# Prompt attention: both heads of a pair in one item, scores in the row halves of TensorE's array, V products alternating between its column halves

## The chip, the cores and the metric

One core of one Trainium2 chip runs the whole program. The metric is the device time of one execution in microseconds; lower is better. Everything is float32. The large projections run as pairs of the faster float32 form (`fp32r`): every number is split into its first bits and the rest, and three products replace one. The products of attention take plain float32 operands; the trace shows one such matmul as two rows, each with a weight load of its own.

## The reference, cut to what matters

Two layers of a streaming encoder are run on 512 prompt frames and on 8 running streams of 16 new frames (the samples). The change touches prompt attention in the second layer: 8 heads of 64 features, every 64-frame chunk attending to itself and to the chunks before it (all 8 of them at most, so over 512 frames the band is the whole causal triangle of chunks), with a bias by relative position.

```python
def band_attention_prompt(q, k, v, rel_bias):
    ...
    scores = jnp.einsum('bcqhd,bckhd->bchqk', chunks(q), kb).astype(jnp.float32) * (D_HEAD_DIM ** -0.5)
    scores = scores + bias.transpose(1, 0, 2, 3)[None].astype(jnp.float32)
    scores = jnp.where((kpos >= 0)[None, :, None, None, :], scores, NEG_INF)
    probs = jax.nn.softmax(scores, axis=-1).astype(v.dtype)
    out = jnp.einsum('bchqk,bckhd->bcqhd', probs, vb)
    return out.reshape(bn, S, D_WIDTH)
```

## The kernel before

All matrix work goes to TensorE. A recorder, `Weave`, runs Python generators and issues their instructions in an order that it works out from estimated TensorE times: a generator yields a number of ns that its next TensorE work has to wait, or an event. Lower priority numbers go first. The tile framework below it may still move an instruction where a buffer isn't free. On the chip each engine takes its instructions in that fixed order.

`odd_mixer` is the second layer's mixer. Its main task (priority 9) projects V, then the pooling inputs, then for each pair of heads j = 0 to 3 K and Q by feature (`kq_proj(j)`: 4 groups of 24 fp32r matmuls with 256 or 384 columns, in `wst`), and then the output projection in two pieces (`out_chunk`: 3 and 5 units of 128 features). Three streams (priority 1) fill in: they take prompt items, and after the event `room` (all K and Q are projected) sample items.

A prompt item before is one head `h` of a pair `j` and one query tile `qt` of 128 frames, 32 items in all, with n = (qt + 1) x 128 keys:

1. scores: one matmul over all 128 rows of the array. `kT` holds both heads' K, 64 features each; `qz` holds Q twice, with the other head's rows zero (L1060, L1061, L1069), so that the product over 128 rows is that of one head;
2. softmax: VectorE adds the bias (up to 256 columns) and takes the maximum, ScalarE takes the exponential and its sum, VectorE scales;
3. qt + 1 transposes of 128 x 128, into the scores' bank, and a copy to `pt` by ScalarE;
4. V products: qt + 1 matmuls with 64 output features, into partitions 64h to 64h + 63 of the pair's bank `pos[j]`, which is a column half of the array.

When a pair's 8 items are done its bank is split into `cat[4 + j]` for the output projection. A sample item has scores and V products in four column strips of 32; its cached K and V (1 MB each) are loaded by SyncE (SP) at L1137 into the pool `xpool` of 7 buffers, in order, each load waiting for a buffer to come free. The eight PSUM banks are shared by all.

Of the kernel before, what the change touches and what calls it, by code (L numbers as in the profile page):

```python
# [10 lines left out]
AF = mybir.ActivationFunctionType  # L11
# [34 lines left out]


class Weave:
    """Issues generators' instructions in the order in which TensorE can take them.

    A generator yields None where another may go on, a number of ns that its next
    TensorE work has to wait, or an Event to wait for.
    """

    def __init__(self):
        self.now = 0.0
# [28 lines left out]


class Ordered:
    """An engine whose instructions keep the program's order while on is set."""

    on = False  # L90

# [14 lines left out]
def trunk_kernel(  # L106
# [57 lines left out]
    def mm(out, lhsT, rhs, start, stop, n, share=1, more=False):  # L164
        fast = lhsT.dtype == F32R
        W.now += PASS * (max(n, 256) if fast else 4 * n / share) + 2
        nc.tensor.matmul(out, lhsT=lhsT, rhs=rhs, start=start, stop=stop, skip_group_check=more)  # L167
# [11 lines left out]
    def bank(shape=(P, 512)):  # L179
        return psp.tile(list(shape), F32, tag="ps", name=nm("ps"))  # L180

    def t4(shape):
        return t4p.tile(list(shape), F32, tag="t4", name=nm("t4_"))

    def t2(shape):
        return t2p.tile(list(shape), F32, tag="t2", name=nm("t2_"))

    def st(n=1):
        return stp.tile([P, n], F32, tag="st", name=nm("st"))
# [17 lines left out]
        return rawp.tile([P, 5, 512], F32, tag="raw", name=nm("raw"))  # L207

    def fetch(srcs):
        """Yields the rows of srcs in turn, loaded two by two."""  # L210
        for i, src in enumerate(srcs):
            if i % 2 == 0:
                w = raw()[:, :4, :].rearrange("p (h a) c -> p h (a c)", h=2)
                nc.sync.dma_start(out=w[:, 0, :], in_=src)
                if i + 1 < len(srcs):
                    nc.sync.dma_start(out=w[:, 1, :], in_=srcs[i + 1])
            yield w[:, i % 2, :]
# [17 lines left out]
        return r  # L235

    class Norm:
        """1 / sqrt(mean of squares + EPS), the squares in one or two parts."""

        def __init__(self):  # L240
            self.ms = None
# [14 lines left out]
            return rsqrt(self.ms)  # L256

    class Normed:
        """The normed rows by feature, each number as its first 12 bits and the rest."""

        def __init__(self, gain):
            self.gain = gain
# [18 lines left out]
            return [x[:, c] for x in self.part(k)]  # L281

    class Quarters:
        """The same in quarters (feature half, row half) and with Winograd's four sums of them."""

        def __init__(self, gain, rows=False):
            self.gain = gain
# [111 lines left out]
    def group_cols(g):  # L399
        return slice(0, GA) if g == 0 else slice(GA, NT)  # L400

    def wst(X, hl, g):
        for t in ((0, 1), (2, 3, 4))[g]:
            yield X.ev[t]
        cols = group_cols(g)
        n = cols.stop - cols.start
        ps = bank()
        for k in range(NK):
            c = slice(k * P, (k + 1) * P)
            xh, xl = X.part(k)  # L410
            mm(ps[:, :n], hl[:, 0, c], xh[:, cols], k == 0, False, n)
            mm(ps[:, :n], hl[:, 0, c], xl[:, cols], False, False, n)
            mm(ps[:, :n], hl[:, 1, c], xh[:, cols], False, k == NK - 1, n)
            if k % 4 == 3:
                yield
        return ps[:, :n]
# [78 lines left out]
        return PostNorm(gpost, src, dst, after if X is not None else None)  # L495

    class Seven:
        """Two units of 128 output features with seven quarter products for eight.

        [A11 A12; A21 A22] times [B11 B12; B21 B22], the rows in halves, the features in  # L500
        halves, and the two units as the two column blocks.
        """

        def __init__(self, one, two, X):
            self.X = X
# [59 lines left out]
                    yield  # L565

    class GateUp(Seven):
        """Gate and up of 128 hidden features and their product."""

        def __init__(self, layer, f, X):  # L570
            super().__init__(wgate[layer, f], wup[layer, f], X)
# [20 lines left out]
            split((self.hid[:, 0, HT:], self.hid[:, 1, HT:]), up)  # L592

    class Units(Seven):
        """Two units by themselves."""

        def __init__(self, one, two, X):
            super().__init__(one, two, X)
# [10 lines left out]
            act.copy(out=self.out[0][:, HT:], in_=a)  # L609

    class Plain:
        """Two units of 128 output features, all eight quarter products as they are."""

        def __init__(self, one, two, X):
            self.X = X
# [95 lines left out]
    def even_mixer(X, hls):  # L711
# [56 lines left out]
        cat = {}  # L768

        def pairs(todo):  # L770
            """The pairs of units in todo, each with its weights made ready before the work on the last."""
            made = []

            def make():
                i, j, _ = todo[len(made)]
                p = (PlainUnits if (i, j) in DIRECT else Units)(ev_t[i], ev_t[j], X)
                p.prepare()
                made.append(p)

            make()  # L780
            for n, (_, _, use) in enumerate(todo):
                yield from made[n].steps()
                if n + 1 < len(todo):
                    make()
                yield from use(*made[n].out)
# [147 lines left out]
    def odd_mixer(X):  # L933
# [121 lines left out]
        def kq_proj(j):  # L1055
            hk = unit(feed)
            hq = unit(feed)
            kT = t2([P, NT])
            qz = t4([P, 2, NP])
            nc.gpsimd.memset(qz[64:128, 0, :], 0.0)  # L1060
            nc.gpsimd.memset(qz[0:64, 1, :], 0.0)  # L1061
            for g in range(2):
                cols = group_cols(g)
                pk = yield from wst(X, hk, g)
                act.copy(out=kT[:, cols], in_=pk)
                pq = yield from wst(X, hq, g)
                for h in range(2):
                    r = slice(64 * h, 64 * h + 64)
                    act.mul(out=qz[r, h, g * GA : (g + 1) * GA], in_=pq[r, :GA], mul=0.125)  # L1069
                    if g == 1:  # L1070
                        dve.tensor_scalar(
                            out=qs[r, j, :, h, :],
                            in0=pq[r, GA:].rearrange("p (b s) -> p b s", s=LS),
                            scalar1=0.125,
                            scalar2=None,
                            op0=ALU.mult,
                        )
            nc.gpsimd.tensor_copy(out=ks[:, j, :], in_=kT[:, NP:])
            nc.sync.dma_start(out=nkp[j], in_=kT[:, :NP])
            nc.sync.dma_start(out=nks[j], in_=ks[:, j, :])  # L1080
            kq[j] = (kT, qz)
            W.signal(kq_ev[j], 1500)

        def prompt_stream(items):
            for j, qt, h in items:
                yield kq_ev[j]
                kT, qz = kq[j]
                hd = 2 * j + h
                n = (qt + 1) * P
                nb_ = min(n, 256)  # L1090
                s = bank()
                mm(s[:, :n], qz[:, h, qt * P : (qt + 1) * P], kT[:, :n], True, True, n)
                dve.tensor_tensor(
                    out=s[:, n - nb_ : n],
                    in0=s[:, n - nb_ : n],
                    in1=bias[hd // 4][:, hd % 4, 256 - nb_ :],
                    op=ALU.add,
                )
                m = row_max([s[:, :n]])
                pr = t2([P, NP])  # L1100
                sm = st()
                act.activation(out=pr[:, :n], in_=s[:, :n], func=AF.Exp, bias=m, accum_out=sm)
                ri = st()
                dve.reciprocal(out=ri, in_=sm)
                dve.tensor_scalar(out=pr[:, :n], in0=pr[:, :n], scalar1=ri, scalar2=None, op0=ALU.mult)
                yield 1800 + 3.2 * n
                for kt in range(qt + 1):
                    flip(s[:, kt * P : (kt + 1) * P], pr[:, kt * P : (kt + 1) * P])
                pt = t2([P, NP])
                act.copy(out=pt[:, :n], in_=s[:, :n])  # L1110
                yield 400 + n
                if j not in pos:
                    pos[j] = bank()
                po = pos[j]
                for kt in range(qt + 1):
                    mm(
                        po[64 * h : 64 * h + 64, qt * P : (qt + 1) * P],
                        vt(kt)[:, hd * 64 : hd * 64 + 64],
                        pt[:, kt * P : (kt + 1) * P],
                        kt == 0,  # L1120
                        kt == qt,
                        P,
                        2,
                    )
                done[j] += 1
                if done[j] == 8:
                    ct = cat[4 + j] = hid_tile()
                    split((ct[:, 0, :NP], ct[:, 1, :NP]), po)
                    W.signal(prompt_done[j], 2000)
                yield  # L1130
# [77 lines left out]
                    W.signal(sample_done, 500)  # L1208
                yield

        prompt_items = iter([(j, qt, h) for j in range(4) for qt in range(4) for h in range(2)])
        sample_items = iter(range(NB))
        room = Event()

        def stream(i):
            yield from prompt_stream(prompt_items)
            yield room
            yield from sample_stream(sample_items)

# [179 lines left out]
```

## Time and profile before

| what | value |
|---|---|
| median of 3 runs | 1335.15 us (1334.96 to 1335.39) |
| span of the profiled execution | 1333.4 us |
| TensorE (PE) busy, share of the span | 1309.9 us, 98% |
| VectorE (DVE) busy | 890.7 us, 67% |
| ScalarE (ACT) busy | 618.5 us, 46% |
| K/Q projections with prompt items, 719 to 798 us | PE busy 78.89 of 79 us |
| rest of attention with the first piece of the output projection, 798 to 857 us | PE busy 57.04 of 59 us |

The span runs from the first to the last instruction of the program; the median is 1.75 us above it. PE's busy time is the union of its matmuls, whose ends are modelled, so what one matmul costs is read from start to start and not from its length.

### The profile page before, as it was taken

The page shows a single profiled execution, that of the slowest core. Times are in us where ns is not written, and L with a number is a line of the kernel's source. Part 1 is how long each engine was busy: PE and PEld are TensorE (multiplying, and loading weights), DVE is VectorE, ACT ScalarE, POOL GpSimd, SP SyncE. Part 2 cuts the span into 40 slices and gives each one's busy share as a digit, 9 for nine tenths or more (in the row PEclk, how much of TensorE's full clock was granted, in tenths as well). Part 3 has the DMA queues.
Part 4 walks back from the last instruction along what each step waited for, and adds up shares of the span by engine and source line. Part 5 has one row for each costly group of instructions (what it writes and reads, how often), then busy time and mean ns, then how long its engine had stood idle before and what let it go on. Part 6 is the DMA issues. An engine that isn't in the chain of part 4 may idle for free.

```text
span 1333.4 us, 20064 instructions
## 1 busy us (share of the span) xinstructions
PE 1309.9 (98%) x8060; PEld 1190.9 (89%) x8060; DVE 890.7 (67%) x1452; ACT 618.5 (46%) x1134; POOL 60.7 (5%) x119
## 2 busy tenths in 40 slices
PE   7999999999999999999999999999999999999997
PEld 5998989989899998998798886789999898998996
DVE  6985779837576674777556446579646575864866
ACT  5644546535253451554434445456545251551551
POOL 2200101000000000001121000010000000000000
PEclk9999999999999999999999999999999999999999
DMA  7212353212122122145346125642312121221233
GB/s 246 72 64 80 105 205 118 97 62 95 64 95 96 63 95 79 64 151 178 138 151 233 68 75 219 248 165 80 127 64 96 62 95 64 96 97 46 96 127 126
DMA packets 45966, 150.12 MB, mean 113 GB/s; under 512 B 6577, under 2 KB 8497, under 8 KB 45873
## 3 DMA queue, kind: packets, MB, share of 16 engines
q1 hardware_dynamic: 45872, 148.84, 30.7%
q8 instruction: 63, 1.03, 0.3%
q14 instruction: 31, 0.25, 0.1%
HBM read 133.57 MB, written 15.26 MB: 112 GB/s over the span
## 4 chain that ended last, share of the span: by engine, by line
PE 86%; DVE 5%; issue 3%; ACT 2%; DMA 2%; POOL 1%; SPq 0%; DVEq 0%; POOLq 0%; ACTq 0%
PE ps L167 85%; DVE t L99 3%; PE ps L171 1%; DMA xbuf<-t 1%; POOL st L234 1%; DMA raw<-in_dram 1%; ACT t L99 1%; DVE q L99 1%; ACT q L99 1%; DVE x L99 1%; DVE st L99 0%; ACT ps L99 0%; ACT f L99 0%; POOL t L751 0%; SPq L380 0%
## 5 line engine op out<-in xcount | busy, mean ns | idle before, releaser
L167 PE MATMUL ps<-x,q 128*128 128x320 f32 (+2 forms) x4884 | 729.2, 310 | 1.2 <-DVE q L99 1.0
L167 PEld LDWEIGHTS ps<-x,q 128*128 128x128 f32 x4884 | 718.0, 188 | 4.9 <-DVE q L99 2.2
L167 PE MATMUL ps<-q,hid 128*128 128x512 f32 x1800 | 417.6, 391 | 0.5 <-DVE hid L99 0.3
L99 ACT CAST q<-raw 128x1024 fp32r<-128x1024 f32 (+1 forms) x278 | 269.8, 978 | 298.3 <-PE ps L167 248.3
L99 DVE TENSOR_TENSOR q<-raw,q 128x1024 fp32r<-128x1024 f32 (+1 forms) x278 | 313.8, 1132 | 136.5 <-ACT q L99 131.7
L167 PEld LDWEIGHTS ps<-q,hid 128*128 128x128 f32 x1800 | 335.4, 188 | 70.4 <-DVE hid L99 1.0
L99 ACT COPY t<-ps 128x320 f32<-128x320 f32 (+3 forms) x304 | 135.6, 452 | 187.7 <-PE ps L167 169.3
L99 DVE TENSOR_TENSOR t<-ps,t 128x512 f32<-128x512 f32 (+2 forms) x164 | 100.2, 614 | 93.7 <-PE ps L167 93.5
L99 DVE TENSOR_TENSOR raw<-raw 128x512 f32<-128x512 f32 (+1 forms) x141 | 121.8, 865 | 11.8 <-DMA raw<-in_dram 9.7
L99 DVE TENSOR_TENSOR t<-t,t 128x512 f32<-128x512 f32 (+4 forms) x107 | 57.8, 550 | 48.4 <-ACT t L99 46.4
L234 POOL TENSOR_TENSOR st<-st,mhalf 128x1 f32<-128x1 f32 x45 | 31.8, 707 | 1002.5 <-DVE st L99 999.1
L99 DVE SCALAR_TENSOR_TENSOR t<-t,st,t 128x512 f32<-128x512 f32 (+1 forms) x60 | 54.5, 925 | 16.5 <-POOL st L234 15.1
L99 ACT ACTIVATE t<-t 128x320 f32<-128x320 f32 (+1 forms) x60 | 40.1, 668 | 44.9 <-issue 26.5
L171 PEld LDWEIGHTS ps<-ident,t 128*128 128x128 f32 x288 | 34.1, 143 | 25.3 <-DVE t L99 10.4
L171 PE MATMUL ps<-ident,t 128*128 128x128 f32 x288 | 43.7, 280 | 13.0 <-DVE t L99 10.5
L99 ACT CAST hid<-t 128x320 fp32r<-128x320 f32 (+1 forms) x96 | 46.0, 483 | 10.3 <-DVE t L99 8.1
L99 DVE TENSOR_TENSOR t<-t 128x320 f32<-128x320 f32 (+3 forms) x90 | 48.8, 542 | 1.4
L167 PE MATMUL ps<-q,x 128*128 128x512 f32 x192 | 47.8, 403 | 1.0 <-DVE st L99 0.8
L99 DVE TENSOR_TENSOR hid<-t,hid 128x320 fp32r<-128x320 f32 (+1 forms) x96 | 48.8, 512 | 0.1
L99 ACT ACTIVATE ps<-t 128x512 f32<-128x512 f32 x40 | 24.1, 602 | 50.9 <-DVE t L99 50.9
L167 PEld LDWEIGHTS ps<-q,x 128*128 128x128 f32 x192 | 36.1, 192 | 10.7 <-DVE q L99 2.3
L99 DVE TENSOR_TENSOR t<-t,ps 128x320 f32<-128x320 f32 x47 | 22.9, 487 | 33.0 <-PE ps L167 33.0
(91 smaller groups left out, 536.5 us busy)
## 6 DMA issues: line engine op xcount, KB each, us to landing
raw<-in_dram SPq DMA_DIRECT2D x184, 512.0 KB, 4.1
x<-in_dram SPq DMA_DIRECT2D x24, 512.0 KB, 6.1
t<-in_dram SPq DMA_DIRECT2D x22, 512.0 KB, 5.3
xbuf<-t SPq DMA_DIRECT2D x15, 512.0 KB, 3.3
t<-xbuf SPq DMA_DIRECT2D x15, 512.0 KB, 3.9
out_dram<-t SPq DMA_DIRECT2D x15, 256.0 KB, 2.0
c<-in_dram SPq DMA_DIRECT2D x4, 512.0 KB, 4.1
fscr<-x SPq DMA_DIRECT2D x2, 768.0 KB, 3.6
```

Of the source, the lines that this page charges most:

```text
L99: ins = op(*args, **kw)
L167: nc.tensor.matmul(out, lhsT=lhsT, rhs=rhs, start=start, stop=stop, skip_group_check=more)
L171: nc.tensor.transpose(out=out, in_=in_, identity=ident)
L234: nc.gpsimd.tensor_tensor(out=r, in0=ms, in1=mhalf, op=ALU.pow)
```

## The change

An item is now a pair `j` and a query tile `qt`, 16 items in all, and two of the three streams take them; the third goes to the samples as soon as `room` is signalled. Q is kept once (`qT`, no zeros), beside K in one buffer. The scores of head h are a matmul over 64 rows of the array, rows 64h to 64h + 63, into a bank of its own: two matmuls one behind the other, each with half of the rows. The V products of the two heads alternate. The transposed probabilities go back over the probabilities (no `pt`). K's sample columns are copied by ScalarE from PSUM, no longer by GpSimd. The estimates that set the order are raised to the pair's.

```diff
         def kq_proj(j):
-            kT = t2([P, NT])
-            qz = t4([P, 2, NP])
-            nc.gpsimd.memset(qz[64:128, 0, :], 0.0)
-            nc.gpsimd.memset(qz[0:64, 1, :], 0.0)
+            both = t4([P, 2, NP])
+            kT, qT = both[:, 0, :], both[:, 1, :]
             for g in range(2):
-                act.copy(out=kT[:, cols], in_=pk)
+                act.copy(out=kT[:, o], in_=pk[:, :GA])
+                if g == 1:
+                    act.copy(out=ks[:, j, :], in_=pk[:, GA:])
                 pq = yield from wst(X, hq, g)
+                act.mul(out=qT[:, o], in_=pq[:, :GA], mul=0.125)
                 for h in range(2):
-                    act.mul(out=qz[r, h, g * GA : (g + 1) * GA], in_=pq[r, :GA], mul=0.125)
-            nc.gpsimd.tensor_copy(out=ks[:, j, :], in_=kT[:, NP:])
...
-            for j, qt, h in items:
+            for j, qt in items:
-                s = bank()
-                mm(s[:, :n], qz[:, h, qt * P : (qt + 1) * P], kT[:, :n], True, True, n)
+                ss = [bank() for _ in range(2)]
+                for h in range(2):
+                    r = slice(64 * h, 64 * h + 64)
+                    mm(ss[h][:, :n], qT[r, qt * P : (qt + 1) * P], kT[r, :n], True, True, n, 2)
...
-                yield 1800 + 3.2 * n
+                yield 2200 + 5 * n
+                for h in range(2):
+                    s, pr = ss[h], prs[h][0]
...
-                pt = t2([P, NP])
-                act.copy(out=pt[:, :n], in_=s[:, :n])
-                yield 400 + n
+                    act.copy(out=pr[:, :n], in_=s[:, :n])
+                yield 600 + 1.5 * n
...
                 for kt in range(qt + 1):
+                    for h in range(2):
+                        hd = 2 * j + h
...
         def stream(i):
-            yield from prompt_stream(prompt_items)
+            if i < 2:
+                yield from prompt_stream(prompt_items)
```

**Place 1, PE, prompt items.** Before, inside pair j = 0: `t2_809` is K and `t4_810` the padded Q of the pair, `ps850` its bank of V products, `t2_861` and `t2_863` the transposed probabilities of two items. One row of this list is one matmul, or as many as it says.

```order
L167 MATMUL ps864_6749<-t2_809_6451,t4_810_6452 128x384
L167 MATMUL ps850_6699<-t2_861_6726,x750_5933 64x128 x2
L167 MATMUL ps850_6699<-t2_863_6745,x750_5933 64x128 x2
L167 MATMUL ps869_6762<-t2_809_6451,t4_810_6452 128x512
L171 MATMUL ps856_6713<-ident_84,t2_858_6718 128x128 x3
```

After, inside pair j = 1: `t4_825` holds Q and K, `t2_893` and `t2_896` the two heads' transposed probabilities.

```order
L167 MATMUL ps902_6973<-t2_893_6914,x750_5933 64x128
L167 MATMUL ps902_6973<-t2_896_6920,x750_5933 64x128
L167 MATMUL ps902_6973<-t2_893_6914,x750_5933 64x128
L167 MATMUL ps902_6973<-t2_896_6920,x750_5933 64x128
L167 MATMUL ps913_7020<-t4_825_6591 128x512
L167 MATMUL ps914_7021<-t4_825_6591 128x512
```

Two heads' V products stood one item behind the other, and only where two items happened to meet; now they alternate in every item, and two score matmuls, of half the rows each, stand together.

**Place 2, VectorE, softmax of an item with 512 keys.** Before (`ps929` is the bank of scores, `x804` the bias):

```order
L99 TENSOR_TENSOR ps929_7060<-ps929_7060,x804_6426 128x256
L99 TENSOR_REDUCE st930_7063<-ps929_7060 128x1
L99 RECIPROCAL st933_7068<-st932_7066 128x1
L99 TENSOR_SCALAR t2_931_7065<-t2_931_7065,st933_7068 128x512
L99 TENSOR_SCALAR t4_805_6440<-ps928_7045 64x8x16
```

After, the same tile of pair j = 1 (`ps913` and `ps914` are the two heads' scores, `raw930` a weight that is split):

```order
L99 TENSOR_TENSOR ps913_7020<-ps913_7020,x804_6426 128x256
L99 TENSOR_TENSOR q932_7118<-raw930_7112,q932_7118 128x1024
L99 TENSOR_REDUCE st915_7025<-ps913_7020 128x1
L99 TENSOR_TENSOR ps914_7021<-ps914_7021,x804_6426 128x256
L99 TENSOR_REDUCE st918_7031<-ps914_7021 128x1
L99 RECIPROCAL st921_7036<-st917_7028 128x1
L99 TENSOR_SCALAR t2_916_7027<-t2_916_7027,st921_7036 128x512
L99 RECIPROCAL st922_7039<-st920_7034 128x1
L99 TENSOR_SCALAR t2_919_7033<-t2_919_7033,st922_7039 128x512
```

One head's chain of four instructions has become two heads' of eight, in one piece.

**Place 3, PE, sample items.** Before (`x1085` is the cached V of stream 2, `x1108` and `x1117` the cached K of streams 4 and 5; stream 3's scores stand some ten rows ahead of these):

```order
L167 MATMUL ps1087_7691<-x1085_7685,t2_1098_7766 32x128 x16
L167 MATMUL ps1087_7691<-x750_5933,t2_1098_7766 32x128 x4
L171 MATMUL ps1077_7653<-ident_84,t2_1097_7758 128x128
L167 MATMUL ps1102_7821<-x749_5925,t4_805_6440 32x16 x4
L167 MATMUL ps1110_7854<-x1108_7848,t4_805_6440 32x512
L171 MATMUL ps1087_7691<-ident_84,t2_1098_7766 128x128
L167 MATMUL ps1110_7854<-x1108_7848,t4_805_6440 32x512 x3
L167 MATMUL ps1111_7855<-x749_5925,t4_805_6440 32x16 x4
L167 MATMUL ps1119_7888<-x1117_7882,t4_805_6440 32x512 x4
```

After (`x1049` is the V of stream 2, `x1060`, `x1069` and `x1078` the K of streams 3, 4 and 5):

```order
L167 MATMUL ps1051_7646<-x1049_7640,t2_1058_7718 32x128 x16
L167 MATMUL ps1051_7646<-x750_5933,t2_1058_7718 32x128 x4
L167 MATMUL ps1062_7759<-x1060_7753,t4_805_6440 32x512 x4
L167 MATMUL ps1063_7760<-x749_5925,t4_805_6440 32x16 x4
L171 MATMUL ps1051_7646<-ident_84,t2_1058_7718 128x128
L167 MATMUL ps1071_7793<-x1069_7787,t4_805_6440 32x512 x4
L167 MATMUL ps1072_7794<-x749_5925,t4_805_6440 32x16 x4
L171 MATMUL ps1042_7603<-ident_84,t2_1057_7685 128x128
L167 MATMUL ps1080_7827<-x1078_7821,t4_805_6440 32x512 x2
```

Stream 3's scores now come behind stream 2's V products, so the buffer that stream 5's K goes to comes free only a few rows ahead of its use.

## Rows read from the trace of the kernel before

**Rows 1.** The page: span, busy engines, the chain that ended last.

```profile
span 1333.4 us, 20064 instructions
...
PE 1309.9 (98%) x8060; PEld 1190.9 (89%) x8060; DVE 890.7 (67%) x1452; ACT 618.5 (46%) x1134; POOL 60.7 (5%) x119
...
PE 86%; DVE 5%; issue 3%; ACT 2%; DMA 2%; POOL 1%; SPq 0%; DVEq 0%; POOLq 0%; ACTq 0%
```

**Rows 2.** Windows: stretch, busy us of each engine (instructions), clock, DMA.

```profile
719.00:798.00 79.00, 78.89 (x491) 64.35 (x490) 39.04 (x108) 34.66 (x96) 2.54 (x7) 1.00 0.27 96
798.00:857.00 59.00, 57.04 (x653) 39.20 (x652) 34.20 (x126) 28.18 (x78) 1.65 (x8) 1.00 0.68 261
```

**Rows 3.** Timeline of PE, 725 to 744 us: start, length, operands, rows merged.

```profile
729.58 0.67 PE L167 MATMUL ps<-t,x 128*64 128x128 f32 x8
730.17 1.12 PE L167 MATMUL ps<-t,t 128*128 128x512 f32 x2
...
731.38 2.33 PE L167 MATMUL ps<-x,q 128*128 128x384 f32 x12
733.54 1.02 PE L167 MATMUL ps<-t,t 128*128 128x512 f32 x2
734.49 0.87 PE L167 MATMUL ps<-t,x 128*64 128x128 f32 x6
735.29 0.98 PE L171 MATMUL ps<-ident,t 128*128 128x128 f32 x7
...
742.31 1.09 PE L167 MATMUL ps<-t,x 128*64 128x128 f32 x8
743.33 0.86 PE L167 MATMUL ps<-x,q 128*128 128x256 f32 x5
```

**Rows 4.** Timeline of PE, 797 to 824 us.

```profile
805.59 0.30 PE L171 MATMUL ps<-ident,t 128*128 128x128 f32 x1 [1.03 <-DVE t L99]
...
812.49 1.88 PE L167 MATMUL ps<-t,t 128*128 128x512 f32 x4
814.30 0.88 PE L167 MATMUL ps<-t,x 128*64 128x128 f32 x10
...
821.57 1.06 PE L167 MATMUL ps<-t,t 128*32 128x512 f32 x8
822.45 0.23 PE L167 MATMUL ps<-x,t 128*32 128x16 f32 x8
```

**Rows 5.** Groups by form, PE, 719 to 857 us: the V products.

```profile
L167 PE MATMUL ps<-t,x 128*64 128x128 f32 x160 | 22.5, 283 | 0.3 <-ACT t L99 0.2
```

**Rows 6.** Groups by form, VectorE, 719 to 817 us: busy us, mean ns of one.

```profile
L99 DVE TENSOR_TENSOR ps<-ps,x 128x256 f32<-128x256 f32 x24 | 10.3, 429 | 17.0 <-PE ps L167 16.4 <-ACT t L99 0.6
L99 DVE TENSOR_TENSOR q<-raw,q 128x1024 fp32r<-128x1024 f32 x5 | 6.1, 1223 | 3.2 <-ACT q L99 3.2
L99 DVE TENSOR_REDUCE st<-ps 128x1 f32<-128x512 f32 x8 | 5.5, 688 | 0.1
L99 DVE RECIPROCAL st<-st 128x1 f32<-128x1 f32 x31 | 5.0, 161 | 11.4 <-ACT t L99 11.2
L99 DVE TENSOR_SCALAR t<-t,st 128x512 f32<-128x512 f32 x7 | 3.4, 484 | 0.2
```

**Rows 7.** Groups by form, ScalarE, 719 to 817 us.

```profile
L99 ACT ACTIVATION_READ_ACCUMULATOR t<-ps,st 128x1 f32 x31 | 6.0, 194 | 0.0
L99 ACT ACTIVATE t<-ps,st 128x512 f32<-128x512 f32 x8 | 5.5, 689 | 11.6 <-DVE st L99 11.6
```

**Rows 8.** Waits of PE, 719 to 857 us: total us, times, longest.

```profile
PE ps L171 <- DVE t L99: 1.0, 1, 1.0
PE ps L167 <- issue: 0.6, 1, 0.6
```

**Rows 9.** Instructions of L1137, the loads of cached K and V.

```profile
L1137 SPq DMA_DIRECT2D x<-in_dram x24: 327/423/614, 794.3 to 842.7; - x24
...
DMA to landing us min/median/max: 3.1/5.6/8.8
```

More of the change, by code (lines that the diff above doesn't have):

```diff
@@ L1057, in kq_proj @@
             hq = unit(feed)
-            kT = t2([P, NT])
-            qz = t4([P, 2, NP])
-            nc.gpsimd.memset(qz[64:128, 0, :], 0.0)
-            nc.gpsimd.memset(qz[0:64, 1, :], 0.0)
+            both = t4([P, 2, NP])
+            kT, qT = both[:, 0, :], both[:, 1, :]
             for g in range(2):
-                cols = group_cols(g)
+                o = slice(g * GA, (g + 1) * GA)
                 pk = yield from wst(X, hk, g)
-                act.copy(out=kT[:, cols], in_=pk)
+                act.copy(out=kT[:, o], in_=pk[:, :GA])
+                if g == 1:
+                    act.copy(out=ks[:, j, :], in_=pk[:, GA:])
                 pq = yield from wst(X, hq, g)
+                act.mul(out=qT[:, o], in_=pq[:, :GA], mul=0.125)
                 for h in range(2):
                     r = slice(64 * h, 64 * h + 64)
-                    act.mul(out=qz[r, h, g * GA : (g + 1) * GA], in_=pq[r, :GA], mul=0.125)
                     if g == 1:
@@ L1077, in kq_proj @@
                         )
-            nc.gpsimd.tensor_copy(out=ks[:, j, :], in_=kT[:, NP:])
-            nc.sync.dma_start(out=nkp[j], in_=kT[:, :NP])
+            nc.sync.dma_start(out=nkp[j], in_=kT)
             nc.sync.dma_start(out=nks[j], in_=ks[:, j, :])
-            kq[j] = (kT, qz)
+            kq[j] = (kT, qT)
             W.signal(kq_ev[j], 1500)
         def prompt_stream(items):
-            for j, qt, h in items:
+            for j, qt in items:
                 yield kq_ev[j]
-                kT, qz = kq[j]
-                hd = 2 * j + h
+                kT, qT = kq[j]
@@ L1089, in prompt_stream @@
                 n = (qt + 1) * P
                 nb_ = min(n, 256)
-                s = bank()
-                mm(s[:, :n], qz[:, h, qt * P : (qt + 1) * P], kT[:, :n], True, True, n)
[L1093 to L1105, printed above, removed]
-                yield 1800 + 3.2 * n
-                for kt in range(qt + 1):
-                    flip(s[:, kt * P : (kt + 1) * P], pr[:, kt * P : (kt + 1) * P])
-                pt = t2([P, NP])
@@ L1110, in prompt_stream @@
-                act.copy(out=pt[:, :n], in_=s[:, :n])
-                yield 400 + n
+                ss = [bank() for _ in range(2)]
+                for h in range(2):
+                    r = slice(64 * h, 64 * h + 64)
+                    mm(ss[h][:, :n], qT[r, qt * P : (qt + 1) * P], kT[r, :n], True, True, n, 2)
+                prs = []
+                for h in range(2):
+                    s, hd = ss[h], 2 * j + h
+                    dve.tensor_tensor(
+                        out=s[:, n - nb_ : n],
+                        in0=s[:, n - nb_ : n],
+                        in1=bias[hd // 4][:, hd % 4, 256 - nb_ :],
+                        op=ALU.add,
+                    )
+                    m = row_max([s[:, :n]])
+                    pr = t2([P, NP])
+                    sm = st()
+                    act.activation(out=pr[:, :n], in_=s[:, :n], func=AF.Exp, bias=m, accum_out=sm)
+                    prs.append((pr, sm))
@@ new lines, in prompt_stream @@
+                for pr, sm in prs:
+                    ri = st()
+                    dve.reciprocal(out=ri, in_=sm)
+                    dve.tensor_scalar(out=pr[:, :n], in0=pr[:, :n], scalar1=ri, scalar2=None, op0=ALU.mult)
+                yield 2200 + 5 * n
+                for h in range(2):
+                    s, pr = ss[h], prs[h][0]
+                    for kt in range(qt + 1):
+                        flip(s[:, kt * P : (kt + 1) * P], pr[:, kt * P : (kt + 1) * P])
+                    act.copy(out=pr[:, :n], in_=s[:, :n])
@@ L1115, in prompt_stream @@
                 for kt in range(qt + 1):
[L1116 to L1124, printed above, removed]
+                    for h in range(2):
+                        hd = 2 * j + h
+                        mm(
+                            po[64 * h : 64 * h + 64, qt * P : (qt + 1) * P],
+                            vt(kt)[:, hd * 64 : hd * 64 + 64],
+                            prs[h][0][:, kt * P : (kt + 1) * P],
+                            kt == 0,
+                            kt == qt,
+                            P,
+                            2,
+                        )
                 done[j] += 1
-                if done[j] == 8:
+                if done[j] == 4:
                     ct = cat[4 + j] = hid_tile()
@@ L1209, in sample_stream @@
                 yield
-        prompt_items = iter([(j, qt, h) for j in range(4) for qt in range(4) for h in range(2)])
+        prompt_items = iter([(j, qt) for j in range(4) for qt in range(4)])
         sample_items = iter(range(NB))
```

## The prediction

> **What bounds the kernel now.** I read the page first: PE is busy for 98% of the span, and the chain that ended last runs through PE for 86% of it [rows 1]. That is an average, so the windows of the stretch that the change touches come next: from 719 to 798 us PE is busy for 78.89 of 79 us, from 798 to 857 us for 57.04 of 59, at a granted clock of 1.00, while VectorE and ScalarE have half of the time free [rows 2]. The view of waits agrees: in these 138 us PE waits for VectorE once, 1.0 us, and 0.6 us for what shows as issue [rows 8]. So here a microsecond off PE is a microsecond off the kernel, as long as PE finds its next operands ready. What a matmul takes is read in the timeline from one start to the next, because the rows overlap.
>
> **What PE pays now.** A plain float32 matmul is two rows. Four score rows of 512 columns and the step behind them take 814.30 - 812.49 = 1.81 us, two take 734.49 - 733.54 = 0.95 [rows 3, 4]: 0.43 us a row, 0.83 ns a column, and 0.09 us for the step out of the full array's shape. One head has 128 + 256 + 384 + 512 = 1280 score columns, eight heads 10,240, two rows each: 17.1 us of scores.
>
> V products have 128 columns and one column half. Eight rows take 743.33 - 742.31 = 1.02 us, six take 735.29 - 734.49 = 0.80 [rows 3]: 0.11 us a row and 0.15 us fixed. With the 0.09 us ahead of them one run of V rows costs 0.24 us beside its work, and I take half of it, 0.12 us, for one change of the array's shape. 160 rows [rows 5] make 17.6 us. Where runs of two heads meet, they already overlap: the eight rows from 729.58 to 730.17, two heads' items one behind the other in the program's order, take 0.59 us against 1.02 for eight rows of one head [rows 3]. That is one row time for two rows, with nothing lost. There are three such places, the first this one, some 0.43 us each: V costs 16.3 us now.
>
> **The change part by part.**
>
> V products alternating between the halves: all 160 rows go two at a time, as they did at 729.58: 8.8 us. **Minus 7.5 us.** The halves of this term are shown by the trace itself; the bounds are 7 and 8.
>
> Scores in the row halves: no row of this trace uses half of the array's rows, so this is bounded. Below: the two heads' rows run one behind the other, each as long as a full one, and nothing is won. Above: they overlap as column halves do [rows 3], and as column strips do in the sample items, where eight rows of 512 columns take 822.45 - 821.57 = 0.88 us, 0.11 each, against 0.43 for a row by itself [rows 4], a full four at a time. A loss below nothing would need a row of 64 contracted numbers to take longer than one of 128; no row suggests it. I take the upper end, since both kinds of column tiles come out at their full factor, across two rows for one matmul: **minus 8.5 us**, between 0 and 8.5.
>
> The Trainium skill has a measured price for row halves' nearest relation: "TensorE: Matmul & The Clock Gate", section "Measured speedup vs the span model", gives 3.07 for four row tiles, not 4. An estimate from it, 1.5 to 1.75 for two, would make the term 5.7 to 7.3 us; no row here shows row tiles, and the column strips above lose nothing.
>
> Changes of the array's shape: the scores used to share the full shape with their neighbours and now need one of their own. But V runs are fewer, and scores often stand directly behind V products (place 1). Counted in the order from the first score to the end of the output projection's first piece there are 80 changes before and 76 after: 4 x 0.12 = **minus 0.5 us**, between -0.5 and +2.5 (if a change to row halves costs twice as much, over some 25 of them).
>
> Softmax of a pair: the same instructions in other groups. For 512 keys VectorE and ScalarE run bias 0.43, maximum 0.69, the second head's 0.43 and 0.69, exponential 0.69, its sum 0.19, reciprocal 0.16, scale 0.48: 3.8 us from score to transpose, 5.0 if a weight's split of 1.22 comes between, as place 2 has it [rows 6, 7]. PE's cover for pair j = 1 is 24 projection rows at (733.54 - 731.38) / 12 = 0.18 us [rows 3], six transposes and twelve V rows, some 6 us. The other pairs of 256 to 512 keys have 5 us or more by the same count. The thinnest is the first item of j = 3: some 3.6 us against about 2.9, with a split of `cat` between. PE already waits there, 1.0 us [rows 4]. I cost the softmax at nothing; uncovered, it would be about 1 us an item.
>
> ScalarE's eight 64-row writes of Q become eight of 128 rows, K's sample columns move to it in four small copies, and GpSimd loses its clearing of `qz` and its copies. ScalarE is idle for more than half of this stretch [rows 2]: nothing. The probabilities' in-place copy waits only for transposes that must be done anyway: nothing.
>
> Samples: 24 loads of 512 KB at L1137 go through seven buffers in order, 5.6 us from issue to landing (3.1 to 8.8) [rows 9]. By place 3 stream 5's K gets the buffer of stream 2's V, which its last products free, and PE then has four short V rows, two score groups of 0.88 [rows 4], two small groups and two transposes, some 2.9 us, before it needs the load: it waits 1.5 to 3 us, and behind it all of PE's queue. Before, stream 3's scores freed that buffer some ten rows earlier. PE had 2 us of waits of its own in this part [rows 2]. **Plus 2.0 us**, between 0 and 4.
>
> Sum: -7.5 - 8.5 - 0.5 + 2.0 = -14.5 us. Against the profiled execution's 1333.4 us that is 1318.9; the median of the runs lies 1.75 us above that span, so the time becomes 1335.15 - 14.5 = **1320.7 us**. Behind 857 us nothing changes but the start, and PE is the bound there too [rows 1], so the gain is kept to the end.
>
> **The rivals.** No change here counts unless it passes 0.2%, 2.7 us, about what a measurement of this kernel can tell.
>
> 1. *The row halves don't overlap* (chance 0.12). All else stands: 1335.15 - 6.0 = 1329.2 us. For it: no row shows row tiles; against it: column tiles overlap fully.
> 2. *They overlap by half* (0.10): if rows start strictly in the program's order, head 1's first row starts with head 0's second, and a pair takes three row times for four rows; scores save 4.3 us: 1324.9. Against it: at 729.58 the first head has four rows ahead of the second's, and all eight are through in 0.59 us [rows 3], which such an order can't give. The Trainium skill ("TensorE: Matmul & The Clock Gate", "Part 3: Packing small matmuls — row/col tiling") says that matmuls start and end strictly in order; by that rule this rival would hold, and the trace disagrees for column tiles.
> 3. *The sample loads become the bound* (0.10): what is saved behind the last projection, about a quarter (one pair in four, 4 us), goes into waits for cached K and V: about 1324.5 us. For it: loads use buffers as they come free and PE's share falls just there [rows 2]; against it: PE has the output projection to fill in, where the order puts it.
> 4. *Slower* (0.07): PE waits ahead of the transposes in every item, for VectorE's scaled probabilities, since two streams of pairs interleave less than three of heads. Its price is the uncovered part of the chain. It decides from 14.5 + 2.7 = 17.2 us on, 1.1 us for each of the 16 items: 1338 us. For it: 3.8 to 5.0 us of chain and a wait that exists already [rows 4, 6, 7]; against it: a cover of 5 us and more in all but a few items.
> 5. *No change* (0.04): scores dearer in the new shape and waits eat the rest: 1334.
>
> **How the numbers follow.** The forecast has the remaining 0.57. Faster are the forecast and rivals 1 to 3, 0.89; within 0.2% is rival 5, 0.04; slower is rival 4, 0.07. The low end, 1316.5, has no sample wait, and most of PE's present waits gone; the high end takes in rivals 1 to 3: 1330.
>
> **What the changed kernel's profile would show.** V rows in runs of 4 to 16, of which eight take 0.59 us. Score rows on 64 x 128, in pairs that start together: two heads' 512 columns in about 0.95 us; 1.4 would be rival 2, 1.8 rival 1. The start of the second piece of the output projection 14 to 15 us earlier. One wait on a load at stream 5's scores. PE's waits for VectorE's `t` ahead of transposes above 5 us in total, or a second stretch of idle PE, would make the prediction wrong.

## The result, and the profile after

The changed kernel takes 1320.74 us (median of four runs, 1320.24 to 1322.09), the kernel before in the same comparison 1335.1: a ratio of 0.9892, with a 95% interval from 0.9878 to 0.9906. Predicted were 1320.7 us, from 1316.5 to 1330. The profiled execution took 1320.24 us, with a span of 1318.5.

The page of the changed kernel: the span, the busy time of each engine, and the engines of the chain that ended last [rows 1].

```profile
span 1318.5 us, 20069 instructions
...
PE 1294.0 (98%) x8060; PEld 1178.4 (89%) x8060; DVE 889.0 (67%) x1452; ACT 614.0 (47%) x1130; POOL 54.9 (4%) x107
...
PE 86%; DVE 5%; issue 3%; ACT 2%; DMA 2%; POOL 1%; SPq 0%; DVEq 0%; POOLq 0%; ACTq 0%
```

PE has as many matmul rows as before and is busy 15.9 us less; the span has shrunk by 14.9. Nothing has taken PE's place as the bound. Next the windows of the changed kernel, of the two stretches that answer to [rows 2]: up to the last K/Q projection, and from there to the end of the sample items (stretch; length, busy us and instructions of PE, PEld, VectorE, ScalarE, GpSimd; granted clock; DMA).

```profile
719.00:782.00 63.00, 63.00 (x461) 53.42 (x460) 37.92 (x108) 32.80 (x93) 0.30 (x1) 1.00 0.33 120
782.00:840.00 58.00, 54.58 (x669) 35.63 (x667) 32.42 (x122) 27.30 (x77) 1.58 (x8) 1.00 0.74 278
```

The first stretch has become 16 us shorter, without a moment of idle PE. The second is only 1 us shorter, and PE's free time in it has grown from 1.96 us [rows 2] to 3.42. The landmarks in the timeline of PE say it more exactly. From the first score row to the last projection row it was 719.05 to 797.45, 78.4 us, and is 718.96 to 781.91, 62.95; from there to the first row of the feed-forward part (before 899.05, after 884.25) it was 101.6 and is 102.3; from there to the end it was and is 434.3. So a gain of 15.4 us lies ahead of the last projection, 0.7 is lost in the middle, and nothing happens behind.

The timeline of PE in the changed kernel answers to [rows 3] (start, length, operands and shapes, rows merged).

```profile
718.96 0.93 PE L167 MATMUL ps<-t 64*128 64x128 f32 x8
719.82 1.35 PE L167 MATMUL ps<-t,x 128*128 128x512 f32 x4
...
741.84 1.09 PE L167 MATMUL ps<-t,x 128*64 128x128 f32 x16
742.87 0.70 PE L167 MATMUL ps<-t 64*128 64x256 f32 x4
743.50 3.14 PE L167 MATMUL ps<-x,q 128*128 128x256 f32 x24
...
752.77 0.66 PE L167 MATMUL ps<-t,x 128*64 128x128 f32 x8
753.35 1.13 PE L167 MATMUL ps<-t 64*128 64x512 f32 x4
754.41 2.36 PE L167 MATMUL ps<-x,q 128*128 128x384 f32 x12
...
759.44 0.88 PE L167 MATMUL ps<-t,x 128*64 128x128 f32 x12
760.25 1.09 PE L171 MATMUL ps<-ident,t 128*128 128x128 f32 x8
...
786.74 0.49 PE L167 MATMUL ps<-t 64*128 64x128 f32 x4
787.17 1.09 PE L167 MATMUL ps<-t,x 128*64 128x128 f32 x16
```

A run of V products of both heads costs 0.58 us for eight rows (753.35 - 752.77), 0.81 for twelve (760.25 - 759.44) and 1.03 for sixteen (742.87 - 741.84); one head's eight rows alone cost 1.02 [rows 3]. The scores of two heads cost 754.41 - 753.35 = 1.06 us for 512 columns, 0.63 for 256, 0.43 for 128. That is 0.83 ns a column and row, the rows of the two heads at once, and 0.21 us besides. The 0.21 us is the price of a run and not of a pair: the items of 128 and 256 columns that stand together at 718.96 take 0.86 us, not 0.43 + 0.63. Groups by form of PE, 719 to 844 us: the V products that answer to [rows 5].

```profile
L167 PE MATMUL ps<-t,x 128*64 128x128 f32 x160 | 12.3, 283 | 0.0
```

And PE's waits in the same stretch, for [rows 8]:

```profile
PE ps L167 <- ACT t L99: 1.9, 2, 1.4
PE ps L167 <- DMA x<-in_dram: 0.7, 1, 0.7
PE ps L171 <- ACT t L99: 0.5, 1, 0.5
PE ps L167 <- DVE hid L99: 0.3, 1, 0.3
```

None of them lies ahead of 782 us, and none is for VectorE's `t`. All belong to the sample items, whose timeline has a second thing to show:

```profile
801.62 1.04 PE L167 MATMUL ps<-t,t 128*32 128x512 f32 x2
802.60 0.33 PE L171 MATMUL ps<-ident,t 128*128 128x128 f32 x1
...
814.99 1.11 PE L167 MATMUL ps<-x,t 128*32 128x512 f32 x16
...
817.06 1.10 PE L167 MATMUL ps<-x,t 128*32 128x512 f32 x12 [0.69 <-DMA x<-in_dram]
818.09 0.96 PE L167 MATMUL ps<-q,hid 128*128 128x512 f32 x3
819.06 1.05 PE L167 MATMUL ps<-x,t 128*32 128x512 f32 x4
820.04 0.96 PE L167 MATMUL ps<-q,hid 128*128 128x512 f32 x3
...
829.01 1.30 PE L167 MATMUL ps<-x,t 128*32 128x128 f32 x40 [1.38 <-ACT t L99]
```

At 817.06 is the load wait that the prediction placed at stream 5's scores, 0.69 us. And groups of strips are torn apart: at 801.62 two rows of 512 columns, one strip of four, take 802.60 - 801.62 = 0.98 us, and four rows take as much at 819.06, while eight rows that stand together cost 0.88 [rows 4]. (The 0.98 holds the step back to the full array behind it, some 0.1 us, the 0.88 does not.) The row at 814.99 is whole: its 16 rows are eight of 512 columns and eight of 16.

Since rows overlap, work is summed here by starts: each PE row counts from its start to the next row's start, by kind, from the first score row to the feed-forward part; a wait counts with the row ahead of it. Of these sums the text below speaks.

| kind | before, us | after, us |
|---|---|---|
| scores (64 rows) | 18.93 | 12.27 |
| V products (160) | 20.42 | 11.15 |
| transposes | 17.4 | 19.0 |
| sample strips (448) | 19.5 | 21.3 |
| all others, the projections above all | 103.8 | 101.6 |
| all | 180.0 | 165.3 |
| of it waits | 2.7 | 3.8 |

### The profile page after: what moved, and what is told of

Its sections match the earlier page's. It is cut to its first block, busy times and chain, and to the rows that moved or that the text cites. A ratio compares the mean times of both kernels' runs of the same rounds, so it can differ in the third digit from the quotient of the medians.

```text
span 1318.5 us, 20069 instructions
## 1 busy us (share of the span) xinstructions
PE 1294.0 (98%) x8060; PEld 1178.4 (89%) x8060; DVE 889.0 (67%) x1452; ACT 614.0 (47%) x1130; POOL 54.9 (4%) x107
## 3 DMA queue, kind: packets, MB, share of 16 engines
q8 instruction: 63, 1.03, 0.3%
## 4 chain that ended last, share of the span: by engine, by line
PE 86%; DVE 5%; issue 3%; ACT 2%; DMA 2%; POOL 1%; SPq 0%; DVEq 0%; POOLq 0%; ACTq 0%
PE ps L167 84%; DVE t L99 3%; PE ps L171 1%; DMA xbuf<-t 1%; POOL st L234 1%; ACT t L99 1%; DMA raw<-in_dram 1%; DVE q L99 1%; ACT q L99 1%; DVE x L99 1%; DVE st L99 0%; ACT ps L99 0%; ACT f L99 0%; POOL t L751 0%; SPq L380 0%
## 5 line engine op out<-in xcount | busy, mean ns | idle before, releaser
L99 ACT COPY t<-ps 128x320 f32<-128x320 f32 (+2 forms) x304 | 135.0, 451 | 193.7 <-PE ps L167 173.8
```

Of the source, the lines that this page charges most:

```text
L99: ins = op(*args, **kw)
```

## The experiments

The theory: both kinds of half tiles overlap fully, and that is the whole gain. Against it stood that the row halves do nothing, that PE starts rows strictly in the program's order, and that the gain comes from the new order of items. Then followed the question where the gain behind the last projection had gone. Each kernel has five runs (e7 four); every diff is against the changed kernel, and kernels are compared by their ratios to the kernel before (0.001 is 1.3 us). The first four shared one chip, the last three another.

**e1: the scores over all 128 rows again**, Q twice with zeros, all else as changed.

```diff
-            both = t4([P, 2, NP])
-            kT, qT = both[:, 0, :], both[:, 1, :]
+            kT = t2([P, NP])
+            qT = t4([P, 2, NP])
+            nc.gpsimd.memset(qT[64:128, 0, :], 0.0)
+            nc.gpsimd.memset(qT[0:64, 1, :], 0.0)
...
-                act.mul(out=qT[:, o], in_=pq[:, :GA], mul=0.125)
+                    act.mul(out=qT[r, h, o], in_=pq[r, :GA], mul=0.125)
...
-                    mm(ss[h][:, :n], qT[r, qt * P : (qt + 1) * P], kT[r, :n], True, True, n, 2)
+                    mm(ss[h][:, :n], qT[:, h, qt * P : (qt + 1) * P], kT[:, :n], True, True, n, 2)
```

> The changed kernel with its scores back over all 128 rows (Q twice, with zeros, as before); pairs, streams, the alternating V products and the order on TensorE stay. Theory (the row halves overlap, so two heads' scores cost one): 8.5 us of score work come back, some 3 us of shape changes go (16 pairs, about 0.2 us each), so 5 to 6 us slower than the changed kernel, 1326 us. Rival (the gain is that of the V products and of fewer, longer runs; the row halves give nothing net, because each pair pays for its shape): 1320 to 1322 us.

Measured: 1326.06 us, ratio 0.9927 (0.9915 to 0.994), 0.0035 or 4.7 us above the changed kernel. The scores' sum is 17.4 us instead of 12.3. The row halves are worth about 5 us, net of the shape change that they cost, near the lower end of the 5 to 6 expected.

**e3: both heads' scores in row half 0.** Head 1's scores are computed from head 0's Q and K.

```diff
-                    mm(ss[h][:, :n], qT[r, qt * P : (qt + 1) * P], kT[r, :n], True, True, n, 2)
+                    mm(ss[h][:, :n], qT[0:64, qt * P : (qt + 1) * P], kT[0:64, :n], True, True, n, 2)
```

> The changed kernel with the score matmuls of both heads in row half 0 (head 1's scores are computed from head 0's Q and K); number, size, shape and order of all instructions stay. Theory (the gain in the scores is the overlap of the two halves): the two run one behind the other, 8.5 us more, 1329 us. Rival (a matmul over 64 rows is cheaper by itself, or the gain is elsewhere): 1320 to 1322 us.

Measured: 1327.97 us, ratio 0.9945 (0.9933 to 0.9958), 7.1 us above the changed kernel. The same pair of 512 columns in e3's timeline:

```profile
757.11 1.98 PE L167 MATMUL ps<-t 64*128 64x512 f32 x4
759.02 2.38 PE L167 MATMUL ps<-x,q 128*128 128x384 f32 x12
```

759.02 - 757.11 = 1.91 us against 1.06: 0.85 more, two further rows at the 0.43 that the prediction took from [rows 4]. At 256 columns it is 1.06 against 0.63. Shape and order are the same in both kernels, so what differs is the overlap alone, and it is complete: two heads in the time of one, plus 0.21 us for the way into and out of the shape. The sum of all scores is 20.2 us, 7.9 more. Of the changed kernel's 12.3, 0.56 is a wait for ScalarE behind the last pair, which e3 does not have; without it the overlap is worth 8.5 us. The time rose by less, because in all e3's PE waits 1.0 us less.

**e5: both heads' V products in column half 0.** Column half 1 of each pair's bank is set to zero, so half of prompt attention's output is left out; four small fills on VectorE are added.

```diff
+                    dve.memset(pos[j][64:128, :], 0.0)
...
-                for kt in range(qt + 1):
-                    for h in range(2):
+                for h in range(2):
+                    for kt in range(qt + 1):
...
-                            po[64 * h : 64 * h + 64, qt * P : (qt + 1) * P],
+                            po[0:64, qt * P : (qt + 1) * P],
```

> The changed kernel with the V products of both heads in column half 0, head 0's and then head 1's, the second over the first; the other half of each pair's bank is set to zero by VectorE (4 small instructions more), so half of prompt attention's output is left out. Theory (the gain in the V products is the overlap of the column halves, 160 rows in 80 row times): 8 to 9 us more, 1329 us. Rival (the gain comes from 16 runs in place of 29 and from the order): 1320 to 1323 us.

Measured: 1328.19 us, ratio 0.9944 (0.9932 to 0.9957), 6.9 us above the changed kernel. The timeline of e5:

```profile
744.04 1.96 PE L167 MATMUL ps<-t,x 128*64 128x128 f32 x16
745.94 0.70 PE L167 MATMUL ps<-t 64*128 64x256 f32 x4
...
756.04 1.09 PE L167 MATMUL ps<-t,x 128*64 128x128 f32 x8
757.06 1.13 PE L167 MATMUL ps<-t 64*128 64x512 f32 x4
```

Sixteen rows take 1.90 us against 1.03, eight 1.02 against 0.58: with one half there is no overlap, as before the change, and the V products' sum is 8.6 us larger, within the 8 to 9 expected. The time rose by less: all the other rows of the stretch together take 1.1 us less than in the changed kernel.

**e2: column halves used, but the heads in turn**, first all of head 0's rows, then head 1's.

```diff
-                for kt in range(qt + 1):
-                    for h in range(2):
+                for h in range(2):
+                    for kt in range(qt + 1):
```

> The changed kernel with the V products of an item in another order: all of head 0's, then all of head 1's, in place of alternating. Theory (TensorE itself starts a row of the free column half past the rows that wait for the other half, as at 729.58 us of the trace before): no difference, 1320 to 1322 us. Rival (rows start strictly in the program's order, so only alternating products overlap): the last row of head 0 overlaps with the first of head 1 and no more; some 7 us slower, 1328 us.

Measured: 1324.38 us, ratio 0.9914 (0.9901 to 0.9928), 2.9 us above the changed kernel. The two intervals overlap, but no run of e2 is below 1323.82 and none of the changed kernel above 1322.09. That is neither of the two expectations, and the timeline shows why:

```profile
743.75 1.58 PE L167 MATMUL ps<-t,x 128*64 128x128 f32 x16
745.26 0.70 PE L167 MATMUL ps<-t 64*128 64x256 f32 x4
...
755.16 0.66 PE L167 MATMUL ps<-t,x 128*64 128x128 f32 x8
755.75 1.13 PE L167 MATMUL ps<-t 64*128 64x512 f32 x4
...
761.84 1.15 PE L167 MATMUL ps<-t,x 128*64 128x128 f32 x12
762.91 1.09 PE L171 MATMUL ps<-ident,t 128*128 128x128 f32 x8
```

Eight rows take 0.59 us, as in the alternating order; twelve take 1.07 instead of 0.81 and sixteen 1.51 instead of 1.03. In the run of sixteen the single rows start, in ns, at 0, 160, 269 and 378, one each; then in twos at 487, 596, 706 and 815; then at 981, 1090, 1199 and 1308, one each. With four rows a head all run in twos, with six a head from head 0's third row on. So PE does not start its rows strictly in the program's order: a row of the other half starts ahead of waiting rows, but past no more than three of them (head 1's first starts within 14 ns of head 0's first, third or fifth, the fourth from its last). A run takes 4 + 2 x (n - 4) row times for n rows a head, 12, 8 and 4 for 8, 6 and 4. Over four pairs that is 4 x (4 + 2) x 0.109 = 2.6 us more, and the V products' sum is 3.05 larger. Alternating is worth that much, and only in items of three and four key tiles. The kernel before shows the same where one head's eight rows are followed by the other's six:

```profile
738.33 1.36 PE L167 MATMUL ps<-t,x 128*64 128x128 f32 x14
739.62 0.66 PE L171 MATMUL ps<-ident,t 128*128 128x128 f32 x4
```

739.62 - 738.33 = 1.29 us is 0.15 fixed and some ten row times for fourteen rows, so only four of the six overlap. Whether the limit counts rows, matmuls or weight loads isn't shown.

**e4: three streams take the pairs**, as many as took heads before.

```diff
-            if i < 2:
+            if i < 3:
```

> The changed kernel with all three streams on prompt items, as before the change: the samples then start only when the prompt items run out. Theory (two streams of pairs already cover the softmax chains, and PE's waits behind the last projection come from the samples): 1319 to 1323 us, no waits less ahead of the last projection, since there are none. Rival (two streams interleave too little, and the time behind the last projection is lost because samples and the last pair share the banks): 2 us or more faster, below 1319 us.

Measured: 1324.97 us, ratio 0.9916 (0.9901 to 0.9931), 3.2 us slower than the changed kernel, which neither expectation had. The two intervals overlap; beside e6 on the same chip, which is as fast as the changed kernel, it is 3.3 us, and the slowest run of e6 (1322.47) is faster than the fastest of e4 (1324.76). From the first score to the last projection it takes 67.0 us instead of 62.95. PE's waits from 719 to 850 us, the three largest:

```profile
PE ps L167 <- issue: 2.0, 1, 2.0
PE ps L171 <- DVE st L99: 1.5, 2, 0.9
PE ps L171 <- DVE t L99: 1.0, 2, 0.8
```

The first lies among the sample items. The two for VectorE stand ahead of transposes inside the prompt items: the kind of wait that the prediction's rival 4 feared comes with three streams, not with two. From the first score to the feed-forward part e4 takes 4.1 us longer, 2.6 of them waits. Why is not settled.

**e6: a larger estimate for the copy ahead of the sample items' V products**, so that the recorder puts more between, where PE waited 1.38 us for ScalarE.

```diff
-                yield 500
+                yield 1200
                 o = s2[:, P : 2 * P]
```

> The changed kernel with one number of the order changed: a sample item's V products are planned 1200 ns behind its transposes, not 500. Theory (behind the last projection the changed kernel gives back what the last pair saves, half of it in PE's waits for ScalarE's copies of transposed probabilities, 1.9 us, which came from an order without cover): 1 to 2 us faster than the changed kernel, 1319 us. Rival (the waits move to the loads of cached K and V, which are the bound there): 1320 to 1322 us.

Measured: 1321.66 us, ratio 0.9888 (0.9872 to 0.9904): no difference. PE's waits from 719 to 843 us, the two largest:

```profile
PE ps L167 <- ACT t L99: 1.2, 2, 0.6
PE ps L167 <- DMA x<-in_dram: 1.0, 1, 1.0
```

The wait of 1.38 us for ScalarE has shrunk to 0.6 (the other 0.6 was there before), but the load wait has grown from 0.7, and with smaller ones PE waits 4.3 us in the stretch instead of 3.8. The waits moved, as the rival had it, and not to the loads alone.

**e7: e6, and an estimate of 5 us for a sample item's loads** ahead of its scores.

```diff
                 kc, vc = load(b, [x10([P, 2, D]) for _ in range(2)])
+                yield 5000
...
-                yield 500
+                yield 1200
```

> As e6_copy_cover, and a sample item's scores are planned 5000 ns behind its loads. Theory (the rest is given back by score matmuls in strips that are torn apart, two strips in place of four at a time, where the order has them ahead of their load): 2 to 3 us faster than the changed kernel, 1318 us; the rows of the strips' 512 columns come in eights. Rival (the loads are the bound): the samples end later and the second piece of the output projection waits for them, 1321 us or more.

Measured: 1317.57 us, ratio 0.9857 (0.9841 to 0.9873). Beside e6 on the same chip that is 4.1 us less; against the changed kernel the ratios give 4.7, and the intervals lie apart. The timeline of e7, then its PE waits from 719 to 843 us:

```profile
815.72 1.11 PE L167 MATMUL ps<-x,t 128*32 128x512 f32 x16
816.76 0.97 PE L167 MATMUL ps<-q,hid 128*128 128x512 f32 x3
...
821.62 1.11 PE L167 MATMUL ps<-x,t 128*32 128x512 f32 x16
822.66 0.96 PE L167 MATMUL ps<-q,hid 128*128 128x512 f32 x3
```

```profile
PE ps L167 <- ACT t L99: 0.6, 1, 0.6
PE ps L171 <- ACT t L99: 0.5, 1, 0.5
PE ps L167 <- DVE hid L99: 0.3, 1, 0.3
```

The load wait is gone, all but one group of the rows of 512 columns stand together in eights (a row x16 has eight of 16 columns too), and the strips' sum is 19.35 us, as before the change (19.5). The feed-forward part starts at 879.69 instead of 884.25. In the profiled executions 1.8 of these 4.6 us are given back behind it (436.1 us to the end instead of 434.3), where PE now waits 1.9 us instead of 0.6, 1.1 of it once for a weight's split on VectorE. A start that comes earlier still found work there that wasn't ready.

## Why the prediction was right

The time and the sum hold, and so does the mechanism: both overlaps are complete, and PE stays the bound. The terms for V products and scores come out as predicted once the fixed time of a run is put where the prediction had it, in the changes of shape. The term for the samples is right in size alone.

*V products, predicted -7.5, bounds 7 and 8.* Measured -9.3 in the sums, outside the bounds. That the halves overlap fully is shown by e5, and by 0.109 us a row that is 16.1 us before (with the three places that overlapped already) and 8.7 after, -7.4. The rest is not overlap: the 160 rows lie in 16 runs instead of 29, and the 0.15 us that a run has fixed is saved 13 times, 1.95 us. That saving stood in another term, the changes of shape, where it was set off against new changes.

*Scores, predicted -8.5; shape changes -0.5.* Measured -6.7 in the sums, -7.2 without the wait of 0.56 us. e3 shows that the overlap itself is complete, 8.5 us. The 1.3 us between is the price of the shape: beside 17.1 us of work the scores paid 1.9 us in 25 runs, where they often shared the full array's shape with their neighbours, and beside 8.5 they pay 3.2 in 15 runs, 0.21 each. So a pair of 512 columns takes 1.06 us and not the 0.95 that was forecast, and with 128 keys the 0.21 uses up what the overlap saves. Set off against the V products' 1.95 that is -0.6 for all changes of shape, predicted -0.5. V and scores with all shape changes together: predicted -16.5, measured -15.9, or -16.5 without the wait. The price of 0.12 us for each of 80 or 76 changes was a guess, half of one run's cost. That its total came out to within 0.2 us is in part luck, since it is the difference of two larger amounts that the prediction did not price apart.

*Rivals 1 and 2.* In e3's terms 1.9 us would have been rival 1 for a pair of 512; the changed kernel has 1.06, and rival 2's 1.4 is out too. The rule in the Trainium skill ("TensorE: Matmul & The Clock Gate", "Part 3: Packing small matmuls — row/col tiling"), that matmuls start strictly in order, disagrees with e2's trace: head 1's first row starts beside head 0's fifth, with three of head 0's rows still ahead of it. The measurement decides; but beyond three waiting rows the order does count, which neither the rule nor my expectation had, though the fourteen rows at 738.33 of the trace before showed it. The estimate from the same page's 3.07 for four row tiles, 5.7 to 7.3 us, happens to hold the 6.7 of the sums (7.2 without the wait), though not the overlap by itself, 8.5 in e3, nor the 4.7 by which e1 is slower, and not for its reason: two row halves show a factor of two, and it is the fixed 0.21 us of a run that is missing.

*The softmax at nothing.* Right: no wait of PE up to 782 us, and the 1.0 us that PE waited ahead of the first item of j = 3 [rows 4] is gone too. Rival 4 is out for two streams, and e4 shows what it would have looked like.

*The samples, +2.0.* The load wait came where it was predicted and is smaller, 0.69 us instead of 1.5 to 3. But the cost was larger than the wait. Of the quarter of the gain behind the last projection, some 4 us, none arrived; the stretch even took 0.7 us more, some 1.3 of which is work from ahead of the projection (20 V rows and 4 transposes of pair 2) that now falls behind it. So about 3.3 us were lost there: 1.1 more of waits, 1.6 more in the strips, the waits left out, and 0.6 in the transposes and projections around them. That is rival 3's result in this stretch, with another cause: not the loads as a bound, since e7 has the same loads and no wait for them, though its last sample item ends at 849 us instead of 841, but an order that puts strips where their loads and copies aren't ready and breaks them up. Over the whole stretch from the first score to the feed-forward part, waits and strips cost 2.6 us, and the other rows beside scores and V products, perhaps because the projections are broken up less, take 0.8 less: together 1.8 us. That this is near the 2.0 predicted is luck, for the prediction had it all as one wait on a load, and that wait is 0.69.

## What to carry to other kernels

Two small matmuls with half the contraction or half the outputs each belong beside each other in the two halves of the array, those of the column halves in turn: here it halved their time in full, except that a run of scores in row halves cost 0.21 us besides, which eats the gain of the smallest. Count runs, not only rows: of the V products' 9.3 us nearly two came from fewer runs, and two pairs of scores in one run pay the 0.21 us once. And after a change that shortens one part, look at what the order puts next to it: a new estimate of a load's time won another 4 us, more than a quarter of what the change itself had won.

## What was not expected of the hardware

Rows for the other column half start ahead of waiting rows of the program's order, but past no more than three (e2: runs of 8, 12 and 16 rows take 4, 8 and 12 row times, in each of the four pairs). Whether the same holds for row halves was not tried. A strip's two rows of 512 columns by themselves cost 0.98 us with the step back to the full array, all four strips' eight rows together 0.88 without it [rows 4]: one strip alone takes as long as four.
